# A decoder trunk on one core: first-stage squares and sums moved off GpSimd, attention values as a Strassen product, and several attention steps moved between engines

## The chip, the cores and the metric

The kernel runs on one core of one Trainium2 chip. The metric is the device time of one launch in microseconds (us); the time before is the median of 3 runs. Engines are called PE (TensorE), DVE (VectorE), ACT (ScalarE), POOL (GpSimd) and SP (SyncE, which here only issues DMAs).

## What is computed

The reference is one layer of a decoder trunk on x of 1024 tokens by 1024 channels, float32. Cut to what matters:

```
h = rmsnorm(x, attn_norm_g)
z = h @ w_in            # u, v of a gated MLP; pooling input; q, k, v of attention
gates = sigmoid(h @ w_gate + b_gate)
y_a = gmlp_mixer(u, v)  # gelu, layernorm of v, causal mixing in chunks of 128
y_b = pool_mixer(...)   # running means over 2, 4, 8, 16 tokens
y_c = diff_attn_mixer(q, k, v)   # 4 heads, two softmaxes each, causal
merged = g_a*(y_a@proj_a) + g_b*(y_b@proj_b) + g_c*(y_c@proj_c)
x = x + merged @ w_out
x = x + conv_ffn(rmsnorm(x, ffn_norm_g))
return rmsnorm(x, final_norm_g)
```

## The kernel before

Activations lie with channels on the partitions: `xt[kt]` holds 128 channels by 1024 tokens, and half `j` is 512 tokens. Every float32 operand of a large product is split into a high part (a cast on ACT) and a low part (a subtraction on DVE, `split`, L95), and each product is three matmuls (`mm3`, L187: high by high, high by low, low by high). Large weight products use the Winograd form of Strassen's algorithm, 7 block products for 8 (`strassen_pair`, L251); its operands on the activation side, T1 to T4, are sums of blocks of h, made by `winograd` (L202) from four in-place subtractions and two splits of 128x1024 for each of four pairs of tiles.

The program is written with a tile library: it orders the instructions of each engine by program order, priority and a timeline of its own, and each engine then works through its list in order. Buffers come from pools: `c2` gives 6 buffers of 128x512, `w4` 13 of 128x1024, `a4` 34, and `pb1` and `pm1` give 6 and 2 banks of PSUM.

- **First stage** (L435 to L477). For each half j: the product for u (`pu`, 48 matmuls of 128x512), the product for v (`v_part`, 96 of 128x256, tokens on the partitions), squares of x (`squares`) and from their sums the row factors 1/rms (`factors`, ending in a copy into R8, L344). `bcast_rows` (L146, on PE) spreads R8 along the partitions into RB. `squares` puts even tiles on POOL, odd tiles on ACT (squares) and DVE (sums).
- **Attention values, layer norm, gating** (L581 to L593). `values` multiplies h by the value weights, tokens on the partitions, in 8 pieces of 48 matmuls of 128x256; between the pieces stand `winograd` (three on POOL, one on DVE), `layer_norm` and `gating`.
- **q, k and pooling** (L594 to L618). `strassen_pair` four times; `store_qk` multiplies q and k by RB (`times_r`, on POOL) and splits them. `pooling` is drawn from inside the second pair; `pool_out` (L576, plain float32 matmuls) follows the last of these pairs.
- **Gates** (L686): 12 pairs. **Attention** (L1130 to L1163): 32 tiles of scores, softmax, transposition and product with the values. As filler between tiles, `merge_ab` makes the 32 products with proj_a and proj_b. ACT copies each from PSUM (L1096), POOL multiplies it by its gate (L1097) and adds the pair (L1099). `load_p` splits its weights with the low part on POOL. `attend` takes sums of squares of its result on DVE (L1032). `scores` takes the row minimum of each of up to two chunks on DVE (L675) and joins the two with a reduction (L681).
- Then follow the output product, the feed-forward part and the final norm, which the change leaves as they are.

Of the kernel before, what the change touches and what calls it, by code (L numbers as in the profile page):

```python
# [13 lines left out]
F32R = mybir.dt.float32r  # L14
# [4 lines left out]
P = 128  # L19
# [28 lines left out]
def trunk_kernel(  # L48
# [147 lines left out]
    class Act:  # L196
# [5 lines left out]
        def winograd(self, xt, j, T4=True, eng=None):  # L202
# [3 lines left out]
            e = eng or nc.gpsimd  # L206
# [117 lines left out]
    def squares(kt, j):  # L324

        k = 2 * j + kt % 2
        src = xt[kt][:, half(j)]
        sq = c2("acc" if kt < 2 else "sq")
        if kt % 2 == 0:
            nc.gpsimd.tensor_tensor(out=sq, in0=src, in1=src, op=ALU.mult)  # L330
        else:
            nc.scalar.activation(out=sq, in_=src, func=AF.Square)
        if kt < 2:
            acc[k] = sq
        else:
            (nc.gpsimd, nc.vector)[kt % 2].tensor_tensor(out=acc[k], in0=acc[k], in1=sq, op=ALU.add)

    def factors(j):
        nc.vector.tensor_tensor(out=acc[2 * j], in0=acc[2 * j], in1=acc[2 * j + 1], op=ALU.add)
        ps = pm1()  # L340
        ss_cols(ps, acc[2 * j], 4, 1, 0)
        t = tiny(4, "ssum")
        nc.vector.tensor_scalar(out=t, in0=ps[:, :4], scalar1=1.0 / D, scalar2=1e-6, op0=ALU.mult, op1=ALU.add)
        nc.vector.tensor_copy(R8[:, 4 * j:4 * j + 4], rsqrt(t, 4, j == 0))  # L344
# [62 lines left out]
    def load_V(c):  # L407
        return [list(load_parts(w_tm[1 + c, j].rearrange("p a b -> p (a b)"), 2, True))[0] for j in range(2)]
# [26 lines left out]
    for j in range(2):  # L435
# [28 lines left out]
        else:  # L464
            w_V = [load_V(c) for c in range(2)]
# [4 lines left out]
        bcast_rows(R8[:, 4 * j:4 * j + 4], 4, RB[:, half(j)], pm1)  # L470
# [981 lines left out]
```

## Time and profile before

| | before |
|---|---|
| median of 3 runs | 1421.71 us (1421.44 to 1428.28) |
| the profiled execution | 1421.06 us |
| its span, first to last instruction | 1419.4 us |
| PE / DVE / ACT / POOL busy in the span | 1355.5 / 984.9 / 652.4 / 621.7 us |
| mean granted clock of TensorE | 0.984 |

Busy times are of one profiled execution. Matmuls overlap in the records, so PE's pace is read from the distance of their starts, not from the length of one.

### The profile page before, as it was taken

To read this page: it belongs to the slowest core of one execution; us is meant where nothing else is said; L and a number is where in the kernel's file an instruction comes from. 1 tells how busy PE (TensorE), PEld (TensorE's weight loads), DVE (VectorE), ACT (ScalarE), POOL (GpSimd) and SP (SyncE) were. 2 spreads that over 40 slices of the span, in tenths; PEclk is the share of its full clock that TensorE was granted. 3 is DMA by queue.
4 is the path that set the end of the run, shared out by engine and by line. 5 is a ranking of instruction groups with operands and counts; after the bars stand their busy time and mean duration, and the time that the engine had idled before them with its cause. 6 is when DMAs were issued, how large, how long until landed. Compare 5 with 4: busy or idle time off the path is not lost. (4 is left out here: it accounts for less than half of the span.)

```text
span 1419.4 us, 17845 instructions
## 1 busy us (share of the span) xinstructions
PE 1355.5 (96%) x6502; PEld 1130.4 (80%) x6502; DVE 984.9 (69%) x1502; ACT 652.4 (46%) x1065; POOL 621.7 (44%) x399
## 2 busy tenths in 40 slices
PE   7799999999999889989989999999999999999996
PEld 6699777888888677778868788888888887888786
DVE  8764676454444889976959766677676668985854
ACT  6442244443434666642567433343434335455461
POOL 6523365555544545442132466666666640102014
PEclk9999999999999999999999999999999999999998
DMA  5232044323336986358796122222222247945753
GB/s 188 96 112 90 30 178 151 132 104 119 120 118 173 287 223 185 105 185 191 185 245 159 52 102 77 90 89 74 90 89 74 75 144 273 305 128 151 215 127 119
DMA packets 78256, 200.46 MB, mean 141 GB/s; under 512 B 8206, under 2 KB 17550, under 8 KB 78168
## 3 DMA queue, kind: packets, MB, share of 16 engines
q1 hardware_dynamic: 67800, 180.44, 38.6%
q0 software_dynamic: 10368, 18.88, 7.9%
q8 instruction: 51, 0.84, 0.2%
q14 instruction: 37, 0.30, 0.1%
HBM read 143.70 MB, written 47.46 MB: 135 GB/s over the span
## 5 line engine op out<-in xcount | busy, mean ns | idle before, releaser
L189 PE MATMUL b<-ft,fw 128*128 128x512 f32 (+1 forms) x1308 | 291.7, 383 | 8.3 <-ACT ft L96 3.1
L189 PEld LDWEIGHTS b<-ft,fw 128*128 128x128 f32 x1308 | 238.9, 188 | 58.3 <-ACT ft L96 3.9
L351 POOL TENSOR_TENSOR F<-F,RB 128x1024 f32<-128x1024 f32 x74 | 206.0, 2785 | 145.9 <-DVE F L260 135.4
L189 PE MATMUL b<-hb,Ah 128*128 128x512 f32 x608 | 190.1, 392 | 0.0
L260 DVE TENSOR_TENSOR F<-b,c 128x512 f32<-128x512 f32 x152 | 100.8, 683 | 112.8 <-ACT c L279 68.7
L189 PE MATMUL b<-T,Sh 128*128 128x512 f32 x504 | 155.7, 389 | 1.9 <-ACT c L270 1.9
L232 POOL TENSOR_TENSOR s<-r 128x512 f32<-128x512 f32 x36 | 57.0, 1584 | 200.8 <-DMA r<-in_w_up 96.6
L189 PEld LDWEIGHTS b<-hb,Ah 128*128 128x128 f32 x608 | 114.5, 189 | 24.6 <-issue 1.0
L97 DVE TENSOR_TENSOR Sl<-s,Sh 128x1024 fp32r<-128x1024 f32 x76 | 114.0, 1500 | 26.2 <-PE b L189 22.1
L97 DVE TENSOR_TENSOR Al<-r,Ah 128x1024 fp32r<-128x1024 f32 x38 | 52.6, 1385 | 98.2 <-issue 77.7
L189 PE MATMUL b<-hb,Al 128*128 128x512 f32 x304 | 119.0, 392 | 0.8 <-DVE Al L97 0.8
L96 ACT CAST Sh<-s 128x1024 fp32r<-128x1024 f32 x76 | 80.0, 1052 | 72.8 <-PE b L189 48.6
L189 PEld LDWEIGHTS b<-T,Sh 128*128 128x128 f32 x504 | 94.6, 188 | 21.9 <-ACT c L270 2.4
L189 PE MATMUL b<-hb,Sh 128*128 128x512 f32 x304 | 95.4, 396 | 3.9 <-DVE F L260 3.9
L189 PE MATMUL b<-T,Sl 128*128 128x512 f32 x252 | 98.1, 389 | 0.0
L96 ACT CAST Ah<-r 128x1024 fp32r<-128x1024 f32 x38 | 40.0, 1053 | 110.4 <-PE b L189 106.7
L96 ACT CAST fw<-fr 128x512 fp32r<-128x512 f32 x90 | 54.7, 622 | 64.9 <-DVE fw L97 29.0
L189 PE MATMUL b<-Tl,Sh 128*128 128x512 f32 x204 | 79.4, 389 | 0.0
L189 PE MATMUL b<-Th,Sh 128*128 128x512 f32 x204 | 78.7, 390 | 0.7 <-ACT c L270 0.7
L189 PE MATMUL b<-Th,Sl 128*128 128x512 f32 x204 | 78.6, 389 | 0.0
L104 POOL DMA_DIRECT2D ssb<-sq x24 | 20.7, 876 | 125.8 <-ACT sq L171 37.8
L97 DVE TENSOR_TENSOR A<-r,A 128x512 fp32r<-128x512 f32 x38 | 74.6, 1964 | 0.9 <-ACT A L96 0.9
(260 smaller groups left out, 2982.8 us busy)
## 6 DMA issues: line engine op xcount, KB each, us to landing
fr<-in_w_down SPq DMA_DIRECT2D x47, 512.0 KB, 4.6
r<-in_w_up SPq DMA_DIRECT2D x42, 512.0 KB, 3.5
r<-in_w_gate SPq DMA_DIRECT2D x24, 512.0 KB, 4.1
g_d<-F SPq DMA_DIRECT2D x24, 512.0 KB, 4.8
act_d<-cv SPq DMA_DIRECT2D x22, 512.0 KB, 2.6
act<-act_d SPq DMA_DIRECT2D x22, 512.0 KB, 6.8
fr<-in_w_out SPq DMA_DIRECT2D x18, 512.0 KB, 4.0
ssb<-sq POOLq DMA_DIRECT2D x24, 256.0 KB, 3.9
```

What stands on the lines that cost most here:

```text
L96: nc.scalar.copy(hi, src)
L97: (eng or nc.vector).tensor_tensor(out=lo, in0=src, in1=hi.bitcast(F32), op=ALU.subtract)
L104: nc.gpsimd.dma_start(out=dst, in_=src, accum_op=ALU.add)
L189: nc.tensor.matmul(ps, lhsT=w[a], rhs=x[b], start=first and i == 0, stop=last and i == 2, skip_group_check=more)
L232: eng.tensor_tensor(out=s1[:, :NH], in0=a21, in1=a22, op=ALU.add)
L260: nc.vector.tensor_tensor(out=o, in0=ps, in1=c, op=ALU.add)
L351: (eng or nc.gpsimd).tensor_tensor(out=F, in0=F, in1=RB, op=ALU.mult)
```

## The change

It joins five edits. (1) `squares` puts all squares on ACT and all sums on DVE; `factors` and `bcast_rows` get high priority. (2) All four `winograd` calls are on DVE and stand ahead of the values. (3) `values` becomes one Strassen product of 7 block products of 48 matmuls, with tokens on the partitions; it shares T1 to T4 with the later pairs and needs sums and splits of the value weights, which DVE and ACT make; `layer_norm` and `gating` stand between its steps. (4) `times_r` of the first three q, k pairs is on DVE, and `pool_out` is drawn from inside the first gate pairs. (5) In attention the gate multiplication reads PSUM on DVE, the sum of a pair is an accumulating DMA, the low part of the projection weights is on DVE, the squares are on ACT, and the minimum is carried from one chunk to the next instead of being reduced.

```diff
-        def winograd(self, xt, j, T4=True, eng=None):
+        def winograd(self, xt, j, T4=True):
-            e = eng or nc.gpsimd
+            e = nc.vector
...
-        if kt % 2 == 0:
-            nc.gpsimd.tensor_tensor(out=sq, in0=src, in1=src, op=ALU.mult)
-        else:
-            nc.scalar.activation(out=sq, in_=src, func=AF.Square)
+        nc.scalar.activation(out=sq, in_=src, func=AF.Square)
...
-            (nc.gpsimd, nc.vector)[kt % 2].tensor_tensor(out=acc[k], in0=acc[k], in1=sq, op=ALU.add)
+            nc.vector.tensor_tensor(out=acc[k], in0=acc[k], in1=sq, op=ALU.add)
...
+        with tc.high_priority():
...
...
+        with tc.high_priority():
+            bcast_rows(R8[:, 4 * j:4 * j + 4], 4, RB[:, half(j)], pm1)
...
+    def values():
+        (a11, a12), (a21, a22) = w_V
...
+        def store(o, banks, c, r, i):
+            for b in range(2):
+                TT(out=o[b], in0=banks[b], in1=c[b], op=ALU.add)
...
+        A11, A12 = operand(a11), operand(a12)
+        b1, b2 = ([pb1() for _ in range(2)] for _ in range(2))
+        prod(b1, A11, "B11", True, True)
+        c1 = copies([c2("v") for _ in range(2)], b1)
+        yield
+        s1, s2 = w4(n="s1"), w4(n="s2")
+        TT(out=s1, in0=a21, in1=a22, op=ALU.add)
+        TT(out=s2, in0=s1, in1=a11, op=sub)
+        prod(b2, A12, "B21", True, False)
+        store(c1, b2, c1, 0, 0)
+        S1 = operand(s1)
+        yield
+        b3 = [pb1() for _ in range(2)]
+        prod(b3, S1, "T1", True, True)
+        S2 = operand(s2)
+        TT(out=a21, in0=a11, in1=a21, op=sub)
+        TT(out=a12, in0=a12, in1=s2, op=sub)
+        yield
+        prod(b1, S2, "T2", False, True)
...
+        prod(b1, S3, "T3", False, True)
...
+        prod(b4, A22, "T4", True, False)
...
+        prod(b3, S4, "B22", False, True)
...
-    values(0, (2, 3))
-    h.winograd(xt, 0)
+    for j in range(4):
+        h.winograd(xt, j)
+    vs = values()
+    next(vs)
     layer_norm()
-    values(1, (2, 3))
-    h.winograd(xt, 1, eng=nc.vector)
-    values(0, (0, 1))
-    h.winograd(xt, 2)
+    next(vs)
+    next(vs)
     gating(0)
-    values(1, (0,))
+    next(vs)
     gating(1)
-    h.winograd(xt, 3)
+    next(vs)
+    next(vs)
     wB = prepare(w_qk[0])
-    values(1, (1,))
+    next(vs)
...
-        store_qk(i, strassen_pair(ops, h, pb1, lambda: next(pl, None)))
+        store_qk(i, strassen_pair(ops, h, pb1, lambda: next(pl, None)), nc.vector)
...
-    for f in range(2):
-        pool_out(f, zb[f])
+    po_ = pool_outs()
...
-        Fs = strassen_pair(w_gate[n_], h, pb1)
+        Fs = strassen_pair(w_gate[n_], h, pb1, lambda: next(po_, None))
...
-            nm_ = tiny(1, "nmx")
-            nc.vector.tensor_reduce(out=nm_, in_=mx, axis=AX.X, op=ALU.min)
...
-        nc.vector.tensor_tensor_reduce(out=junk[:, :P], in0=o, in1=o, scale=1.0, scalar=0.0, op0=ALU.mult,
-                                       op1=ALU.add, accum_out=H["ss"][:, i:i + 1])
+        nc.scalar.activation(out=junk[:, :P], in_=po[:, :P], func=AF.Square, accum_out=H["ss"][:, i:i + 1])
...
-    def load_p(m, g, eng=nc.gpsimd):
+    def load_p(m, g, eng=nc.vector):
...
-                    t = c2("pc")
-                    nc.scalar.copy(t, ps)
-                    nc.gpsimd.tensor_tensor(out=g[:, half(j)], in0=t, in1=g[:, half(j)], op=ALU.mult)
+                    nc.vector.tensor_tensor(out=g[:, half(j)], in0=ps, in1=g[:, half(j)], op=ALU.mult)
                     if (g, j) == (gb, 1):
-                        nc.gpsimd.tensor_tensor(out=ga, in0=ga, in1=gb, op=ALU.add)
+                        accumulate(ga, gb)
```

Three places in the engines' lists show how the order moves. The first is DVE before, at the end of the first half's row factors (`hb` are low parts of h, `acc` sums of squares, `rs` the steps of the reciprocal root, `R_93` the table R8):

```order
L317 SCALAR_TENSOR_TENSOR hb_355<-x_92,cs,hb_355 128x512
L336 TENSOR_TENSOR acc_437<-acc_437,sq_490 128x512
L124 RECIPROCAL rs_48_326<-rs_49_327 128x4
L339 TENSOR_TENSOR acc_429<-acc_429,acc_437 128x512
L129 SCALAR_TENSOR_TENSOR rs_49_327<-rs_48_326 128x4
L130 TENSOR_TENSOR rs_49_327<-rs_49_327,ssum_324 128x4
L131 SCALAR_TENSOR_TENSOR rs_48_326<-rs_49_327,rs_48_326 128x4
L344 COPY R_93<-rs_48_326 128x4
```

and the same place now, where the in-place sums for T1 to T4 (`x`) stand between the steps:

```order
L209 TENSOR_TENSOR x_90<-x_90,x_86 128x512
L208 TENSOR_TENSOR x_87<-x_91,x_87 128x512
L212 TENSOR_TENSOR x_89<-x_89 128x512
L130 TENSOR_TENSOR rs_49_327<-rs_49_327,ssum_324 128x4
L212 TENSOR_TENSOR x_90<-x_90 128x512
L208 TENSOR_TENSOR x_88<-x_92,x_88 128x512
L209 TENSOR_TENSOR x_91<-x_91,x_87 128x512
L131 SCALAR_TENSOR_TENSOR rs_48_326<-rs_49_327,rs_48_326 128x4
L209 TENSOR_TENSOR x_92<-x_92,x_88 128x512
L212 TENSOR_TENSOR x_91<-x_91 128x512
L342 COPY R_93<-rs_48_326 128x4
```

Ahead of the copy into R8 DVE's list now holds 15 of these sums and 14 sums of squares, where it held one and 8 (with 16 of `hb`, 8 of the weights' low parts of 128x256 and 2 of 128x1024 both times).

The second place is PE, where `bcast_rows` (`m_407`) waits for that table. Before, it stood inside the second half's product for u:

```order
L189 MATMUL b_421<-hb_343,wh_109 128x512 x2
L189 MATMUL b_421<-hb_343,wl_110 128x512
L189 MATMUL b_422<-hb_343,wh_115 128x512
L146 MATMUL m_407<-ident,R_93 128x128 x4
L189 MATMUL b_422<-hb_343,wh_115 128x512
L189 MATMUL b_422<-hb_343,wl_116 128x512
L189 MATMUL b_421<-hb_346,wh_109 128x512 x2
```

Now it stands behind the whole of it:

```order
L189 MATMUL b_421<-hb_355,wh_109 128x512 x2
L189 MATMUL b_421<-hb_355,wl_110 128x512
L189 MATMUL b_422<-hb_355,wh_115 128x512 x2
L189 MATMUL b_422<-hb_355,wl_116 128x512
L146 MATMUL m_407<-ident,R_93 128x128 x4
L385 MATMUL m_515<-oh_512,rb 4x512
L189 MATMUL b_558<-wh_183,hb_334 128x256
```

What follows it is the product for v of the second half (`b_558`), whose banks come free when ACT has read those of the first half.

The third is DVE now, in the values' stage (`Tl` low parts of T1 to T4, `vg` the v of the gated MLP in its layer norm, `ya` gating, `wl_1055` the low part of the operand of the fifth block product):

```order
L599 TENSOR_TENSOR vg_123<-vg_123,wk_501 128x1024
L599 TENSOR_TENSOR vg_124<-vg_124,wk_501 128x1024
L639 TENSOR_TENSOR ya_977<-m_974,wk_501 64x256 x2
L639 TENSOR_TENSOR ya_984<-m_981,wk_501 64x256 x2
L639 TENSOR_TENSOR ya_991<-m_988,wk_501 64x256 x2
L639 TENSOR_TENSOR ya_998<-m_995,wk_501 64x256 x2
L639 TENSOR_TENSOR ya_1061<-m_1058,wk_501 64x256 x2
L97 TENSOR_TENSOR Tl_736<-x_92,Th_735 128x1024
L639 TENSOR_TENSOR ya_1068<-m_1065,wk_501 64x256 x2
L639 TENSOR_TENSOR ya_1075<-m_1072,wk_501 64x256 x2
L97 TENSOR_TENSOR wl_1055<-wr_495,wh_1054 128x1024
```

The last of the eight splits, `Tl_736`, which the fourth block product needs, stands behind the layer norm and five of eight gating steps; on PE 164 matmuls of the block products stand between the end of the product for v and the first that reads it. Before, no matmul of `values` needed any T.

## Rows read from the trace of the kernel before

**Rows 1.** The page, part 1: busy us, share of the span, instructions of each engine.
```profile
PE 1355.5 (96%) x6502; PEld 1130.4 (80%) x6502; DVE 984.9 (69%) x1502; ACT 652.4 (46%) x1065; POOL 621.7 (44%) x399
```
**Rows 2.** Stretches: length; busy us (instructions) of PE, PEld, DVE, ACT, POOL; clock; DMA.
```profile
0.00:38.80 38.80, 31.09 (x172) 26.33 (x173) 32.17 (x32) 27.39 (x45) 24.96 (x23) 0.91 0.50 172
38.80:76.10 37.30, 30.04 (x172) 24.87 (x171) 27.47 (x51) 13.92 (x25) 14.64 (x14) 0.91 0.32 102
76.10:129.60 53.50, 53.50 (x423) 52.64 (x423) 32.03 (x60) 19.28 (x31) 17.82 (x13) 1.00 0.37 112
...
460.00:640.00 180.00, 159.68 (x925) 135.11 (x924) 151.90 (x486) 112.43 (x272) 83.47 (x54) 0.96 0.68 198
```
**Rows 3.** Waits of PE over the span: us in total, times, longest.
```profile
PE m L146 <- DVE R L344: 7.2, 1, 7.2
PE sc L672 <- DVE mx L675: 5.5, 4, 2.6
...
PE m L576 <- issue: 2.6, 1, 2.6
```
**Rows 4.** Timeline of PE: start us, us, instruction, xcount, [idle before <-releaser].
```profile
18.27 0.79 PE L189 MATMUL b<-hb,wh 128*128 128x512 f32 x1 [4.67 <-DVE hb L317]
...
26.78 0.40 PE L189 MATMUL b<-wh,hb 128*128 128x256 f32 x2
...
27.14 0.40 PE L189 MATMUL b<-wh,hb 128*128 128x256 f32 x2
...
51.19 2.05 PE L146 MATMUL m<-ident,R 128*128 128x128 f32 x8 [7.18 <-DVE R L344]
```
**Rows 5.** DVE instructions by tile, 0 to 60 us: duration ns min/median/max, starts.
```profile
L336 DVE TENSOR_TENSOR acc<-acc,sq x6: 679/1772/1787, 10.7 to 43.7; 128x512 f32<-128x512 f32 x6
...
L317 DVE SCALAR_TENSOR_TENSOR hb<-x,cs,hb x16: 739/1524/1786, 4.9 to 43.0; 128x512 fp32r<-128x512 f32 x16
```
**Rows 6.** Timeline of DVE: the copy into R8, first half and second half.
```profile
49.85 1.19 DVE L344 COPY R<-rs 128x4 f32<-128x4 f32 x1
...
74.71 0.17 DVE L344 COPY R<-rs 128x4 f32<-128x4 f32 x1
```
**Rows 7.** Timeline of ACT at the first gelu.
```profile
57.09 1.28 ACT L427 ACT_TABLE_LOAD   x1
58.39 1.57 ACT L427 ACTIVATE vg<-b,R 128x256 f32<-128x256 f32 x4
```
**Rows 8.** Groups of DVE by form, 60 to 135 us: busy us, mean ns.
```profile
L97 DVE TENSOR_TENSOR Tl<-x,Th 128x1024 fp32r<-128x1024 f32 x8 | 9.9, 1251 | 7.2 <-PE b L189 5.8 <-ACT Th L96 1.0 <-DMA y_d<-uT 0.4
L568 DVE TENSOR_TENSOR ya<-m,wk 64x256 f32<-64x256 f32 x16 | 6.8, 422 | 6.5 <-PE m L561 6.3
L528 DVE TENSOR_TENSOR vg<-vg,wk 128x1024 f32<-128x1024 f32 x4 | 4.6, 1228 | 0.0
...
L523 DVE TENSOR_SCALAR vg<-vg,mv,rs 128x256 f32<-128x256 f32 x8 | 2.7, 413 | 0.0
```
**Rows 9.** Stretches with a lower clock (columns as in rows 2).
```profile
160.00:170.00 10.00, 7.39 (x28) 5.00 (x26) 9.85 (x13) 4.02 (x5) 5.82 (x4) 0.93 0.00 0
170.00:180.00 10.00, 10.00 (x41) 7.95 (x40) 7.06 (x5) 1.64 (x2) 7.44 (x3) 0.90 0.00 0
```
**Rows 10.** Groups of DVE, 460 to 640 us: busy us, mean ns.
```profile
L1002 DVE SCALAR_TENSOR_TENSOR sc<-sc,nr,sc 128x1024 f32<-128x1024 f32 (+3 forms) x16 | 22.1, 1384 | 0.2
L1032 DVE CUSTOM_DVE_ANT_0 sq<-O 128x128 f32<-128x128 f32 x32 | 17.0, 533 | 5.3 <-ACT O L1029 5.3
L1001 DVE SCALAR_TENSOR_TENSOR nr<-nr,s,nlam 128x1 f32<-128x1 f32 x32 | 12.8, 401 | 0.6
L1002 DVE SCALAR_TENSOR_TENSOR sc<-sc,nr 128x256 f32<-128x256 f32 (+3 forms) x16 | 11.3, 713 | 0.4
...
L681 DVE TENSOR_REDUCE nmx<-mx 128x1 f32<-128x2 f32 x32 | 4.7, 148 | 0.1
...
L1122 DVE TENSOR_TENSOR gc<-sc,gc 128x512 f32<-128x512 f32 x3 | 2.1, 689 | 1.0 <-PE sc L189 1.0
```

More of the change, by code (lines that the diff above doesn't have):

```diff
@@ L335, in squares @@
         else:
-            (nc.gpsimd, nc.vector)[kt % 2].tensor_tensor(out=acc[k], in0=acc[k], in1=sq, op=ALU.add)
+            nc.vector.tensor_tensor(out=acc[k], in0=acc[k], in1=sq, op=ALU.add)
     def factors(j):
[L339 to L344, printed above, removed]
+        with tc.high_priority():
+            nc.vector.tensor_tensor(out=acc[2 * j], in0=acc[2 * j], in1=acc[2 * j + 1], op=ALU.add)
+            ps = pm1()
+            ss_cols(ps, acc[2 * j], 4, 1, 0)
+            t = tiny(4, "ssum")
+            nc.vector.tensor_scalar(out=t, in0=ps[:, :4], scalar1=1.0 / D, scalar2=1e-6, op0=ALU.mult, op1=ALU.add)
+            nc.vector.tensor_copy(R8[:, 4 * j:4 * j + 4], rsqrt(t, 4, j == 0))
     def gain(kt):
@@ L405, in load_wide, with load_V @@
         return wk, wsm, pbd
-    def load_V(c):
-        return [list(load_parts(w_tm[1 + c, j].rearrange("p a b -> p (a b)"), 2, True))[0] for j in range(2)]
+    def load_V():
+        r = [[w4(n="wr") for _ in range(2)] for _ in range(2)]
+        for c, k in ((0, 0), (0, 1), (1, 0), (1, 1)):
+            nc.sync.dma_start(out=r[c][k], in_=w_tm[1 + c, k].rearrange("p a b -> p (a b)"))
+        return r
     def evac_fm(dst, ps, j):
@@ L464, in trunk_kernel @@
         else:
-            w_V = [load_V(c) for c in range(2)]
+            w_V = load_V()
             wk, wsm, pbd = load_wide()
@@ L469, in trunk_kernel @@
             pv = [v_part(1, 0)]
-        bcast_rows(R8[:, 4 * j:4 * j + 4], 4, RB[:, half(j)], pm1)
+        with tc.high_priority():
+            bcast_rows(R8[:, 4 * j:4 * j + 4], 4, RB[:, half(j)], pm1)
         u_gelu(j, pu)
@@ L596, in trunk_kernel, with store_qk @@
         times_r(z, nc.vector)
-    def store_qk(i, Fs):
+    def store_qk(i, Fs, eng=None):
         for n_, F in enumerate(Fs):
-            times_r(F)
+            times_r(F, eng)
             hi, lo = a4(dt=F32R, n="qh"), a4(dt=F32R, n="ql")
@@ L613, in trunk_kernel, with pool_outs @@
             pl = pooling(zb)
-        store_qk(i, strassen_pair(ops, h, pb1, lambda: next(pl, None)))
+        store_qk(i, strassen_pair(ops, h, pb1, lambda: next(pl, None)), nc.vector)
     for _ in pl:
         pass
-    for f in range(2):
-        pool_out(f, zb[f])
+    def pool_outs():
+        for f in range(2):
+            for _ in range(2):
+                yield
+            pool_out(f, zb[f])
+    po_ = pool_outs()
     def load_head(hd):
@@ L675, in scores @@
             nc.vector.tensor_tensor_reduce(
-                out=sc_[:, c0:c0 + n], in0=ps[:, :n], in1=H["T"][:, o:o + n], scale=1.0, scalar=3.0e38,
+                out=sc_[:, c0:c0 + n], in0=ps[:, :n], in1=H["T"][:, o:o + n], scale=1.0,
+                scalar=mx[:, 0:1] if n_ else 3.0e38,
                 op0=ALU.add, op1=ALU.min, accum_out=mx[:, n_:n_ + 1])
-        nm_ = mx[:, 0:1]
-        if len(chunks) > 1:
-            nm_ = tiny(1, "nmx")
-            nc.vector.tensor_reduce(out=nm_, in_=mx, axis=AX.X, op=ALU.min)
+        nm_ = mx[:, n_:n_ + 1]
         sum_ = H["s0"][:, i:i + 1] if c == 0 else tiny(1, "s1")
```

62 lines of the change are left out of this document (47 added, 15 removed).

## Prediction, written before the changed kernel ran

> **What bounds the kernel now.** I read the page's busy shares first. PE works 96% of the span [rows 1], so time comes only from matmuls left out, from places where PE idles, and from stretches with a low clock. A table of stretches [rows 2] says where these are: from the start to the end of the product for v (76.1 us) PE is busy 61.1 of 76.1 us at a clock of 0.91; the values' stage to 129.6 us is solid, PE busy all 53.5 us at full clock; the attention stretch (460 to 640 us) leaves 20.3 of its 180 us idle, with DVE busy 151.9. The list of PE's waits [rows 3] names the places that the change touches: 7.2 us for the table R8, 2.6 us ahead of `pool_out`, 5.5 us in four waits for row minima. PE's timeline [rows 4] dates two: 4.67 us until 18.27 for a low part of h, and 7.18 us until 51.19, where `bcast_rows` wants R8. From it comes PE's pace as well: three matmuls of 128x256 start in 0.36 us (26.78 to 27.14), 0.12 each; one of 128x512 I count as two.
>
> Why DVE is late there shows in its own rows [rows 5]: adding squares to a sum takes 0.68 us at best and 1.77 us in the median, the low part of h 0.74 to 1.79. Even the tiny copy into R8 takes 1.19 us in the first half and 0.17 in the second [rows 6]. POOL is busy 25 of the first 38.8 us, 14.6 of the next 37.3 [rows 2]; I read the long ones as DVE waiting on POOL's accesses to SBUF.
>
> **Part 1, start to the end of v.** DVE's list ahead of R8 now has 16 low parts of h at 0.74 (11.8), 8 low parts of weights of 128x256 at about 0.41 (3.3; L523 has that size [rows 8]), 2 of 128x1024 at 1.25 (2.5), 14 sums of squares at 0.68 (9.5), 15 sums for T1 to T4 at 0.68 (10.2) and some 5 tiny steps at 0.17 (0.9): 38.2 us, at the prices that DVE has without POOL, whose squares, sums and T1 to T4 all leave this stage. It starts at 4.9 [rows 5]; with 3 us of waiting for x and ACT (8 more squares there, some 5 us beside 41 busy of 76 [rows 2]) R8 is ready near 46. PE starts its first half's product 3 us sooner (the low parts come at 0.74 instead of 1.5), ends it near 23, then makes v of one half (96 x 0.12 = 11.5) and u of the other (48 x 0.24 = 11.5), and wants R8 near 46. The wait of 7.2 goes; 4.67 becomes about 1.5. What is late next: v of the second half needs banks that ACT frees with its gelu, behind R8: spreading and copy 1.3, table load 1.28 and two pairs of gelu 0.8 [rows 7], 3.4 us together, which did not show before because u's last matmuls stood behind `bcast_rows`. Then 96 matmuls with the small ones of the factors, 14.5. End of v: 46 + 3.4 + 14.5 = 64 instead of 76.1: **-12**. Ends: 0 if R8 comes 12 us late, -16 if nothing of the 3.4 shows.
>
> **Part 2, the values.** 7 x 48 matmuls for 8 x 48: 48 x 0.12 = 5.8 us saved if nothing else stopped PE. But before, no matmul here needed T1 to T4; now the fourth block product needs the last low part, which stands behind in DVE's list: from the end of v, the second half's factors (4.2, tiny steps and what stands between), statistics of v (2.3), u times RB (1.3), two additions for a stored block (1.4), eight splits (9.9), layer norm (2.7 + 4.6), five pairs of gating (10 x 0.42 = 4.2), all by [rows 8] where they have a row there, and some 2 of tiny steps: about 32 us. PE has 164 matmuls before it (19.7), the spreading (0.6) and seven gating products (4.7): 25 us. So PE waits about 7 us in pieces, and with pieces of idleness comes a lower clock; from 160 to 180 us, behind a hole of 2.6, the granted clock was 0.93 and 0.90 [rows 9], a mean between the two levels of 1.2 and 2.4 GHz, which cost 0.7 + 1.0 = 1.7 us. I put 1 on it. -5.8 + 7 + 1 is **+2**. Ends: -5.8, nothing waited for; and +11, if every split also waits for its cast on ACT (8 x 1.05 for them beside the 32).
>
> **Part 3, q, k and pooling.** `times_r` of six tensors of 128x1024 goes to DVE at 1.23 (a multiplication of that size [rows 8]), 7.4 us in a stage where DVE is far from full; POOL loses as many. `pool_out` between block products no longer stands in a row that nothing prepared: its wait of 2.6 [rows 3] and the low clock behind it, 1.7, go: **-4**. Ends: 0 and -4.3. The sums of value weights that DVE and ACT make lie beside PE's 25 us.
>
> **Part 4, attention.** DVE loses 32 squares (17.0) with their reads (some 2.6), 32 joins of minima (4.7) [rows 10]; it gains 32 gate multiplications of 128x512 from PSUM at 0.69 (L1122 is one such [rows 10]), 22 us, and 8 low parts at 0.69, 5.5. Its balance by count is +3. POOL, however, loses nearly all its 83.5 us of this stretch [rows 2], and what DVE pays for POOL can be read: L1001 on one column takes 401 ns where tiny steps take 170 [rows 6], 32 x 0.23 = 7.4; L1002 takes 22.1 + 11.3 = 33.4 us for 16 + 16 instructions whose eight lengths of 128 to 1024 columns add up to 18,432 columns, that is 36 times 512; at 0.69 each [rows 10] 25, so 8 less at least, 16 if the smaller tensors were inflated most. DVE would be busy 151.9 + 3 - 20 = 135 of 180 us. ACT sheds 32 copies and gains 32 squares, about nothing. PE idles here because DVE delivers late: I take 9 of the 20.3 us back, near half, since the waits for minima (5.5) and some others end at DVE but a chain of small steps stays: **-9**. Ends: 0 and -20.
>
> Here the Trainium skill speaks against the change: its page Perfetto Trace Analysis, section Optimizing Scalar/DVE Operations, says that moving work between GPSIMD and DVE might not help, as they share a port to SBUF, and that DVE's access costs some 125 ns on PSUM against 60 ns on SBUF. By that the 32 multiplications from PSUM would cost 2 us more, an estimate from that page. The trace shows 689 ns for L1122 from PSUM and 679 for a sum from SBUF, which leaves no such difference. That the port is held by one engine at a time (page SBUF - State Buffer, section SBUF: two separate sides) agrees with 679 against 1772.
>
> **Sum.** -12 + 2 - 4 - 9 = -23. The profiled execution took 1421.06 us around a span of 1419.4, 0.65 below the median of the runs, 1421.71. So about **1398 us**. The order after attention is the same, and I count nothing there.
>
> **Rivals.** (a) The values run free: the splits come in time, because DVE falls idle before the end of v and pulls them forward. Then part 2 is -5.8 and the time 1390. For it: DVE does 9.9 us of splits in 53 now and waits 7.2 for PE there [rows 8]. Against: layer norm stands ahead in the list. 0.15. (b) Attention gains nothing, as DVE's 32 added multiplications take what POOL gives back: 1398 + 9 = 1407. For it: the balance by count is +3, and the relief is inferred. This is also what the skill's rule on offloading would give. 0.20. (c) R8 is as late as before, since 29 sums stand ahead of it: a wait of 7.2 remains, 1405. For it: ACT must scale all of x before those sums can be made. 0.10. (d) Slower: DVE becomes the bound in attention. Each of the 32 products with proj_a and proj_b then holds its bank until DVE comes to it, and PE stands for it as it stands now for a row minimum, 5.5 / 4 = 1.4 us a time [rows 3]: 32 x 1.4 = 44 us over (b), 1451. It decides once DVE has over about 165 us of work in 180; it has 151.9 now, 155 by count if POOL's absence gives nothing. 0.06. (e) Gains and waits cancel, 1415 to 1422: 0.04.
>
> **How the numbers follow.** My forecast has 0.45. The range that should hold 8 in 10 runs from 1384 (case (a) with the better ends of parts 1 and 4) to 1414 (case (b) with half of part 1 lost); it leaves out (d), (e) and the far ends. About 0.5%, 7 us here, is what a measurement of this kernel can tell from no change. Faster by more than that (below 1414.6) are the forecast, (a), (b) and (c) except for their bad ends: 0.86; within it, (e) and some of (b): 0.07; slower, (d) and some sum of bad ends: 0.07.
>
> **What would show it.** Right: the wait for R8 gone and the product for v ended near 64; sums on DVE at 0.68 throughout the first 45 us; 528 matmuls of 128x256 in v and values instead of 576; new waits of PE in 64 to 100 for `Tl`, `vg` and `ya` of some 7 us; DVE near 135 us busy in the attention stretch, its L1001 near 0.2, and PE's idle time there near 11. Wrong: a wait at `bcast_rows` of several us (part 1), waits of PE for the merge's multiplications (part 4), a clock below 0.95 over the values' stage (part 2), or time moved in the stages behind attention, which I left at nothing.

## The result and the profile after

The median is 1402.22 us in 4 runs (1400.68 to 1405.20) for 1421.58 of the kernel before. The medians lie 19.4 us apart; the ratio over all the runs of both is 0.9855 (95% interval 0.9822 to 0.9889). The forecast was 1398. The profiled execution took 1400.68 us, its span 1399.0. Its busy time by engine, for [rows 1]:

```profile
PE 1347.8 (96%) x6454; PEld 1120.9 (80%) x6454; DVE 962.8 (69%) x1481; ACT 654.0 (47%) x1110; POOL 502.3 (36%) x327
```

POOL lost 119 us, PE 8. Where the 20.4 us of the span went is read from the time at which PE reaches the same instruction in both kernels. PE's instructions by tile give it (the two numbers ahead of the semicolon are the first and the last start), here of the kernel after:

```profile
L516 PE MATMUL b<-wh,hb x4: 283/283/363, 62.7 to 72.2; 128*128 128x256 f32 x4
...
L189 PE MATMUL b<-hb,Ah x608: 389/389/478, 119.3 to 1150.2; 128*128 128x512 f32 x152
...
L189 PE MATMUL b<-Th,Sl x204: 388/389/389, 123.9 to 450.9; 128*128 128x512 f32 x102
...
L189 PE MATMUL b<-ft,fw x1308: 277/389/502, 656.7 to 1385.5; 128*128 128x512 f32 x174, 128*128 128x256 f32 x13
```

and of the kernel before:

```profile
L189 PE MATMUL b<-hb,Ah x608: 387/389/1415, 129.5 to 1166.1; 128*128 128x512 f32 x152
...
L189 PE MATMUL b<-Th,Sl x204: 388/389/397, 132.7 to 461.9; 128*128 128x512 f32 x102
...
L189 PE MATMUL b<-ft,fw x1308: 278/389/502, 670.1 to 1405.4; 128*128 128x512 f32 x174, 128*128 128x256 f32 x13
```

The first `b<-hb,Ah` opens the first q, k pair, the last `b<-Th,Sl` is the end of the q, k and gate pairs, the first `b<-ft,fw` opens the output product. The differences (the first two stages part at 76.1 before, at 62.7 after):

| stage | before | after | difference | forecast |
|---|---|---|---|---|
| start to the end of v | 76.1 | 62.7 | -13.4 | -12 |
| values | 53.4 | 56.6 | +3.2 | +2 |
| q, k, pooling, gates | 332.4 | 331.6 | -0.8 | -4 |
| attention and merge | 208.2 | 205.8 | -2.4 | -9 |
| output product to the end | 749.3 | 742.3 | -7.0 | 0 |

So the total came close, but its terms failed in opposite directions: 10 us that were forecast for pooling and attention did not come, and 7 came where none were counted.

The stretches, for [rows 2] (length; busy us and instructions of PE, PEld, DVE, ACT, POOL; clock; DMA):

```profile
0.00:62.70 62.70, 56.68 (x338) 48.57 (x339) 45.65 (x91) 42.06 (x69) 2.90 (x10) 1.00 0.45 157
62.70:119.30 56.60, 51.65 (x378) 48.33 (x377) 41.85 (x76) 25.22 (x40) 11.57 (x12) 0.97 0.31 103
...
451.00:528.00 77.00, 61.56 (x335) 49.22 (x333) 57.98 (x157) 40.79 (x106) 7.09 (x4) 0.91 0.88 245
528.00:612.00 84.00, 82.14 (x515) 70.83 (x514) 75.94 (x254) 58.85 (x181) 4.30 (x5) 1.00 0.75 194
```

The first stage runs at full clock with POOL out of it. The values' stage, solid before, has 5 us of PE idle and a clock of 0.97. Attention falls in two: an opening of 77 us with 15.4 us of PE idle and a clock of 0.91 (1.2 GHz for a part of it), and the rest, nearly solid. PE's longest waits, for [rows 3]:

```profile
PE b L189 <- DVE F L260: 8.0, 2, 6.6
PE m L647 <- DVE F L622: 3.6, 1, 3.6
PE mm L189 <- ACT ph L96: 3.2, 1, 3.2
PE m L632 <- DVE vg L599: 2.9, 1, 2.9
```

The wait for R8 is gone, and so are the row minima from the head of the list. In their place stand 6.6 us at a bank that DVE's sum `F` frees, 3.6 us in `pool_out`, 2.9 us for `vg`, which are taken apart below, and 3.2 us for `ph` in the merge. PE's timeline at each:

```profile
44.68 1.05 PE L146 MATMUL m<-ident,R 128*128 128x128 f32 x8
...
48.56 0.39 PE L189 MATMUL b<-wh,hb 128*128 128x256 f32 x1 [1.88 <-ACT vg L428]
...
87.87 5.38 PE L632 MATMUL m<-wpp,vg 128*128 128x256 f32 x16 [2.94 <-DVE vg L599]
93.43 1.99 PE L632 MATMUL m<-wpp,vg 128*128 128x256 f32 x8 [0.18 <-DVE ya L639]
95.57 1.10 PE L632 MATMUL m<-wpp,vg 128*128 128x256 f32 x4 [0.15 <-DVE ya L639]
97.37 0.39 PE L189 MATMUL b<-wh,Tl 128*128 128x256 f32 x1 [0.69 <-DVE Tl L97]
...
158.49 3.78 PE L647 MATMUL m<-F,wpp 128*128 128x512 f32 x4 [3.61 <-DVE F L622]
...
457.95 1.22 PE L189 MATMUL b<-hb,Sh 128*128 128x512 f32 x2 [6.64 <-DVE F L260]
...
509.00 2.07 PE L189 MATMUL mm<-yv,ph 128*128 128x512 f32 x4 [3.18 <-ACT ph L96]
```

### The profile page after: what moved, and what is told of

It is laid out like the page before. It is cut to its first block, busy times and chain, and to the rows that moved or that the text cites. A ratio compares the mean times of both kernels' runs of the same rounds, so it can differ in the third digit from the quotient of the medians.

```text
span 1399.0 us, 17655 instructions
## 1 busy us (share of the span) xinstructions
PE 1347.8 (96%) x6454; PEld 1120.9 (80%) x6454; DVE 962.8 (69%) x1481; ACT 654.0 (47%) x1110; POOL 502.3 (36%) x327
## 4 chain that ended last, share of the span: by engine, by line
PE 38%; DVE 6%; DMA 3%; issue 2%; ACT 1%; POOL 0%; DVEq 0%; SPq 0%; ACTq 0%; POOLq 0%
PE b L189 38%; DMA fr<-in_w_down 1%; DMA x<-in_xT 1%; DVE fw L97 1%; DMA act<-act_d 1%; DVE Sl L97 0%; DMA x_d<-x 0%; DVE T L97 0%; DVE ft L97 0%; DVE x L908 0%; DVE hb L999 0%; DVE x L1326 0%; ACT fw L96 0%; DVE Al L97 0%; DVE fr L879 0%
## 5 line engine op out<-in xcount | busy, mean ns | idle before, releaser
L349 POOL TENSOR_TENSOR F<-F,RB 128x1024 f32<-128x1024 f32 x68 | 192.3, 2830 | 125.6 <-DVE F L260 124.0
L97 DVE TENSOR_TENSOR Al<-r,Ah 128x1024 fp32r<-128x1024 f32 x38 | 50.0, 1315 | 151.5 <-issue 75.7
L189 PEld LDWEIGHTS b<-hb,Ah 128*128 128x128 f32 x608 | 114.0, 188 | 23.6
L97 DVE TENSOR_TENSOR Sl<-s,Sh 128x1024 fp32r<-128x1024 f32 x76 | 96.5, 1270 | 6.8 <-ACT Sh L96 6.7
L97 DVE TENSOR_TENSOR A<-r,A 128x512 fp32r<-128x512 f32 x38 | 79.6, 2094 | 0.0
L189 PEld LDWEIGHTS b<-hb,Sh 128*128 128x128 f32 x304 | 58.5, 193 | 22.4 <-DVE F L260 8.8
```

What stands on the lines that cost most here:

```text
L97: (eng or nc.vector).tensor_tensor(out=lo, in0=src, in1=hi.bitcast(F32), op=ALU.subtract)
L189: nc.tensor.matmul(ps, lhsT=w[a], rhs=x[b], start=first and i == 0, stop=last and i == 2, skip_group_check=more)
L349: (eng or nc.gpsimd).tensor_tensor(out=F, in0=F, in1=RB, op=ALU.mult)
```

## The experiments

### The first stage alone, and POOL's part in it

The first kernel is that of before with edit 1 of the change and, of edit 2, `winograd` on DVE (its calls stay between the pieces of the values), and nothing else.

```diff
-            e = eng or nc.gpsimd
+            e = nc.vector
...
-        if kt % 2 == 0:
-            nc.gpsimd.tensor_tensor(out=sq, in0=src, in1=src, op=ALU.mult)
-        else:
-            nc.scalar.activation(out=sq, in_=src, func=AF.Square)
+        nc.scalar.activation(out=sq, in_=src, func=AF.Square)
...
-            (nc.gpsimd, nc.vector)[kt % 2].tensor_tensor(out=acc[k], in0=acc[k], in1=sq, op=ALU.add)
+            nc.vector.tensor_tensor(out=acc[k], in0=acc[k], in1=sq, op=ALU.add)
...
+        with tc.high_priority():
...
```

> The kernel before, with the first stage alone changed: all squares on ACT, all sums of squares and all of T1 to T4 on DVE, priority for the factors and the spreading; values, pooling and attention as before. Theory: POOL's accesses made DVE's work two to three times longer there, and taking them away ends the product for v 13.4 us sooner; nothing later gives it back, so 1421.5 - 13.4 = 1408 us (1406 to 1411). Rival: most of the gain is in what the rest of the change does with T1 to T4, and the values' stage, which now has DVE busy with the sums, gives 5 us or more back: 1413 to 1418.

Measured: 1409.05 us, 0.9917 of before (0.9892 to 0.9942). It opens its first q, k pair at 117.9 us, 11.6 sooner than before, and the stages behind it keep their lengths within a few us. The gain of part 1 of the prediction stays; none of it needs the rest of the change. The three things that this kernel joins (squares and sums off POOL, `winograd` off POOL, priority for the factors) were not run apart.

Is it POOL's accesses that made DVE slow, or that the two shared tiles? The next two kernels are the changed one with work on POOL that touches nothing else, and DVE, ACT and PE lists that are the same to the row.

```diff
+    junk_ = a4(n="jk")
+    nc.gpsimd.memset(junk_, 1.0)
+    for _ in range(24):
+        nc.gpsimd.tensor_tensor(out=junk_[:, :NH], in0=junk_[:, NH:], in1=junk_[:, NH:], op=ALU.mult)
```

> The changed kernel with 24 products of 128x512 added on POOL at the start, each reading and writing a buffer that nothing else uses; the lists of DVE, ACT and PE are the same to the row. Theory: POOL's accesses to SBUF alone make DVE's instructions with two inputs from SBUF two to three times longer: over the first 35 us the sums of squares and the low parts of h take 1.5 to 1.8 us instead of 0.7, R8 comes 8 us or more later, and the kernel takes 1410 us (1406 to 1415). Rival: before, DVE was slow because it shared tiles with POOL (squares to add, sums to wait for), which this kernel does not do: 1400 to 1404, sums at 0.7.

```diff
+    for _ in range(48):
+        nc.gpsimd.memset(junk_[:, :NH], 2.0)
```

> The changed kernel with 48 fills of 128x512 (memset) added on POOL at the start, which write a buffer that nothing else uses and read none; lists of DVE, ACT and PE the same to the row. Theory: what slowed DVE in the run with 24 products on POOL (first stage 14 us longer) was POOL reading SBUF through a port that it shares with DVE; fills only write, and DVE's sums stay at 0.68 to 0.8 us: 1400 to 1405. Rival: any work of POOL on SBUF holds the port, and the sums take 1 us or more while it lasts: 1407 to 1420, according to how long the fills last.

Measured: 1415.68 us with the products (0.9965 of before, 0.9947 to 0.9983), just above the theory's range, and 1402.76 with the fills (0.9887, 0.9848 to 0.9925), the changed kernel's own time. DVE's sums of squares and POOL's added work by tile (duration in ns min/median/max, first and last start), with the products:

```profile
L333 DVE TENSOR_TENSOR acc<-acc,sq x12: 682/1103/1525, 13.7 to 48.0; 128x512 f32<-128x512 f32 x12
...
L375 POOL TENSOR_TENSOR jk<-jk x24: 1040/1366/1371, 2.3 to 32.5; 128x512 f32<-128x512 f32 x24
```

with the fills:

```profile
L333 DVE TENSOR_TENSOR acc<-acc,sq x12: 672/682/778, 10.5 to 34.1; 128x512 f32<-128x512 f32 x12
...
L375 POOL MEMSET jk<- x48: 524/526/534, 2.3 to 29.7; 128x512 f32 x48
```

and in the changed kernel:

```profile
L333 DVE TENSOR_TENSOR acc<-acc,sq x12: 678/682/779, 10.9 to 34.2; 128x512 f32<-128x512 f32 x12
```

Products on POOL, on data that nobody else uses, take back all of part 1: the first q, k pair opens at 133.0 us, later than before the change (129.5). PE loses the time at the low parts of h, which DVE makes (median 1056 ns for 742 in the changed kernel), and at `bcast_rows` it does not wait:

```profile
PE b L189 <- DVE hb L317: 11.5, 3, 8.8
```

Fills (48 x 526 ns, 25 us in all, for 33 us of products) do nothing at all. What the second theory named holds: a reading POOL instruction holds DVE up, a writing one does not. The Trainium skill says so (SBUF - State Buffer, section SBUF: two separate sides): an instruction of DVE with two inputs from SBUF and a GpSimd instruction that reads SBUF exclude each other for their whole length. These two runs agree with it.

### The opening of attention

Why does PE wait 6.6 us at 457.95? ACT's timeline of the changed kernel:

```profile
448.19 0.30 ACT L773 ACTIVATE lam<-lam,zero 128x2 f32<-128x2 f32 x1
455.00 1.04 ACT L96 CAST yv<-yr 128x1024 fp32r<-128x1024 f32 x1 [6.51 <-DMA yr<-y_d]
455.95 0.58 ACT L279 COPY c<-b 128x512 f32<-128x512 f32 x1
```

and DVE's:

```profile
456.07 1.23 DVE L97 TENSOR_TENSOR yv<-yr,yv 128x1024 fp32r<-128x1024 f32 x1 [7.21 <-ACT yv L96]
457.22 0.68 DVE L260 TENSOR_TENSOR F<-b,c 128x512 f32<-128x512 f32 x1
```

A cast for the merge (`yv`, the split of y_a) stands in ACT's list ahead of the copy `c` of the last q, k pair. Its data come by a DMA at 455.0, so ACT stands 6.5 us, the copy with it, behind it DVE's sum `F`, and PE at the bank that `F` frees. The next kernel holds the cast back:

```diff
-        nc.scalar.copy(c_3, b1)
+        MK["c3"] = nc.scalar.copy(c_3, b1)
...
-            yab = [load_yab(i) for i in range(4)]
+            with tc.issue_after(MK["c3"].ins):
+                yab = [load_yab(i) for i in range(4)]
```

> The changed kernel, with one thing held back: the splits of y_a and y_b for the merge (yv) stand on ACT and DVE behind the last copy of c_3 in the last q, k pair, instead of ahead of it. Theory: at the opening of attention ACT stands 6.5 us at a cast of yv whose data are not there, the copy of c_3 queues behind it, DVE's sum F behind that, and PE waits 6.6 us for the bank, with a low clock behind the hole (0.91 over 451 to 528 us). Then this kernel has no such wait and takes about 1402 - 6.6 - 2 = 1393 us (1390 to 1397). Rival: the opening is short of work anyway, and the later casts only move the hole to the merge's first products: 1400 to 1404.

Measured: 1389.35 us, 0.9783 of before (0.9764 to 0.9803; the interval of the changed kernel ends above it, at 0.9822), 12.9 under the median of the changed kernel. The copy now stands first (lines are 2 higher in this kernel):

```profile
452.03 0.59 ACT L281 COPY c<-b 128x512 f32<-128x512 f32 x1 [2.87 <-PE b L191]
452.51 1.05 ACT L98 CAST yv<-yr 128x1024 fp32r<-128x1024 f32 x1
```

and attention takes 193.3 us for 205.8. That is 4 us more than the wait and the clock that were expected to go: the two stretches of attention, to be held against those of the changed kernel above,

```profile
452.00:530.00 78.00, 72.25 (x414) 61.45 (x415) 69.18 (x198) 51.43 (x137) 10.28 (x6) 0.93 0.95 268
530.00:612.00 82.00, 80.27 (x490) 68.30 (x488) 67.91 (x222) 53.96 (x166) 4.63 (x6) 1.00 0.77 211
```

show PE with 10.7 us more of work done in the opening (72.25 in 78 us for 61.56 in 77), at a clock of 0.93. Beside the wait for `F`, which fell to 1.40 us, the 3.18 for `ph` at 509.00 is gone too; it stood in the same opening and was not counted.

### Part 5 with the opening mended

Against this kernel the worth of part 5 of the change (part 4 of the prediction) can be measured. The first kernel takes all of it back, the second the merge alone (its gate multiplications, pair sums and the low part of its weights).

Both:

```diff
-    def load_p(m, g, eng=nc.vector):
+    def load_p(m, g, eng=nc.gpsimd):
...
-                    nc.vector.tensor_tensor(out=g[:, half(j)], in0=ps, in1=g[:, half(j)], op=ALU.mult)
+                    t = c2("pc")
+                    nc.scalar.copy(t, ps)
+                    nc.gpsimd.tensor_tensor(out=g[:, half(j)], in0=t, in1=g[:, half(j)], op=ALU.mult)
...
-                        accumulate(ga, gb)
+                        nc.gpsimd.tensor_tensor(out=ga, in0=ga, in1=gb, op=ALU.add)
```

The first alone:

```diff
-                scalar=mx[:, 0:1] if n_ else 3.0e38,
+                scalar=3.0e38,
...
+            nc.vector.tensor_reduce(out=nm_, in_=mx, axis=AX.X, op=ALU.min)
...
-        nc.scalar.activation(out=junk[:, :P], in_=po[:, :P], func=AF.Square, accum_out=H["ss"][:, i:i + 1])
+        nc.vector.tensor_tensor_reduce(out=junk[:, :P], in0=o, in1=o, scale=1.0, scalar=0.0, op0=ALU.mult,
+                                       op1=ALU.add, accum_out=H["ss"][:, i:i + 1])
```

> The changed kernel with y_a's and y_b's splits held back, and with the attention of before: copy by ACT, gate multiplication, sum of a pair and low part of the projection weights on POOL, squares on DVE, minimum joined by a reduction. Theory: with the opening mended, part 5 of the change is worth the difference between the attention stretches of the two kernels, 208.2 - 193.3 = 15 us: 1389.4 + 14 = 1403 us (1399 to 1407), DVE's steps of one column back from about 0.2 to 0.4 us. Rival: the mended opening makes up most of it, and part 5 alone is worth under 5 us: 1390 to 1394.

> The changed kernel with y_a's and y_b's splits held back, and only the merge as before (copy by ACT, multiplication, sum and low part of the projection weights on POOL); squares stay on ACT, the minimum stays carried. Theory: what helps is POOL's absence from SBUF, not the instructions that DVE is spared: DVE loses 32 multiplications here and still gets slower per instruction, 1389.4 + 10 = 1399 us (1396 to 1404). Rival: it is the chain, which the squares and the joins of the minimum made longer, and this kernel keeps it short: 1389 to 1392.

Measured: 1412.91 us with all of part 5 taken back (0.9942 of before, 0.9924 to 0.9961) and 1416.69 with the merge alone (0.9966, 0.9950 to 0.9983). So against the old attention part 5 is worth 23.6 us, more than either theory gave, and all of it is the merge: with that on POOL, squares on ACT and the carried minimum gain nothing (1416.69 with them, 1412.91 without). A part of the 23.6 is not the price of part 5 as such: the old attention takes 215.7 us here for 208.2 in the kernel before, with 13.9 us of waits for row minima for 5.5; why, no run shows. DVE's groups over attention, with the merge on DVE (the kernel with the mended opening; busy us, mean ns),

```profile
L1080 DVE SCALAR_TENSOR_TENSOR sc<-sc,nr,sc 128x1024 f32<-128x1024 f32 (+3 forms) x16 | 17.3, 1082 | 0.2
...
L1171 DVE TENSOR_TENSOR gb<-mm,gb 128x512 f32<-128x512 f32 x16 | 11.0, 687 | 0.7 <-PE mm L191 0.4
...
L1079 DVE SCALAR_TENSOR_TENSOR nr<-nr,s,nlam 128x1 f32<-128x1 f32 x32 | 6.9, 216 | 0.5
```

and with the merge on POOL:

```profile
L1080 DVE SCALAR_TENSOR_TENSOR sc<-sc,nr,sc 128x1024 f32<-128x1024 f32 (+3 forms) x16 | 23.0, 1436 | 0.4
L1079 DVE SCALAR_TENSOR_TENSOR nr<-nr,s,nlam 128x1 f32<-128x1 f32 x32 | 21.3, 665 | 0.8
```

The step on one column takes 665 ns for 216 in the mean. By tile (duration in ns min/median/max) and in time, with the merge on POOL:

```profile
L1078 DVE RECIPROCAL nr<-s x32: 147/159/165, 462.3 to 611.5; 128x1 f32<-128x1 f32 x32
L1079 DVE SCALAR_TENSOR_TENSOR nr<-nr,s,nlam x32: 206/220/2154, 463.4 to 611.6; 128x1 f32<-128x1 f32 x32
...
503.74 3.36 POOL L1175 TENSOR_TENSOR ga<-ga,gb 128x1024 f32<-128x1024 f32 x1
...
504.77 0.15 DVE L1078 RECIPROCAL nr<-s 128x1 f32<-128x1 f32 x1
504.96 2.15 DVE L1079 SCALAR_TENSOR_TENSOR nr<-nr,s,nlam 128x1 f32<-128x1 f32 x1
```

The median is 220 ns, as with the merge on DVE; 14 of the 32 take 333 to 2154 ns. Each of these 14 began while a product or a pair sum ran on POOL and ended 14 to 19 ns after that one's end. The reciprocal just ahead, with one input, never takes over 165 ns, though POOL works beside 15 of the 32. So DVE's step with two inputs from SBUF waits for the end of the POOL instruction that runs. In the kernel before all its 8 long steps (425 to 1315 ns) end 16 to 21 ns after the end of a POOL product as well.

These steps stand in the chain from the scores to the transposition that PE waits for, and their 14 us are the largest growth of any group of DVE. Attention is 21.0 us longer with the merge on POOL (214.3 for 193.3), and 13.8 of them are idle time of PE (21.4 us for 7.6). That DVE's steps make the greater part of it is argued: PE's waits there end at several instructions of DVE and ACT, and ACT too has more to do, 32 copies (127.8 us busy for 113.2), which no run separates from POOL's part. The 32 multiplications that DVE makes in return (687 ns each, 22 us) are not in that chain.

### The values and their buffer

Why do the layer norm and the gating stand ahead of `Tl_736` in DVE's list? T1 to T4, the blocks of h, x, `uT`, `vg` and two tables share one pool of 34 buffers; counted, the last low part is the 35th. It has a place only when the gating of the first half is stored. The next kernel gives the pool one more, paid for by the small buffers.

```diff
-    cp = ctx.enter_context(tc.tile_pool(name="cp", bufs=6))
+    cp = ctx.enter_context(tc.tile_pool(name="cp", bufs=4))
...
-    ap_ = ctx.enter_context(tc.tile_pool(name="ap", bufs=34))
+    ap_ = ctx.enter_context(tc.tile_pool(name="ap", bufs=35))
```

> The changed kernel with one more buffer of 128x1024 in the pool that holds T1 to T4 (35 for 34, paid for by 4 instead of 6 small buffers of 128x512). Theory: the last low part stands behind layer norm and five gating steps on DVE because it has no buffer before the gating of the first half has been stored; with a buffer, DVE's list has all eight low parts ahead of the layer norm, PE's seven gating products no longer stand in front of the fourth block product, and the values' stage (56.6 us, 5 of them waits and 5 more in gating products that wait for banks) takes about 52: 1402 - 4.6 = 1397.6 us (1395 to 1400). Rival: DVE's sum of work is the limit whatever its order, and the waits come back at the sums of the value weights: 56 us and 1401 to 1404.

Measured: 1392.90 us, 0.9808 of before (0.9787 to 0.9828). The list has the eight low parts ahead of the layer norm, and the first q, k pair opens at 104.1 us for 119.3: 15 us, not 5. From the opening of the output product to that of the feed-forward part it takes 114.1 us for 103.9, however, so I gave the buffer a pool of its own that ends with the last q, k pair, once alone and once with the opening of attention mended:

```diff
+    cpool.append(st1.enter_context(tc.tile_pool(name="cp1", bufs=4, reuse_waits="tile")))
+    tx = st1.enter_context(tc.tile_pool(name="tx", bufs=1, reuse_waits="tile"))
...
-                t4, t2 = op2(u, a4, "T")
+                t4, t2 = op2(u, a4, "T", tlow if j == 3 else None)
...
     st1.close()
+    cpool.append(ctx.enter_context(tc.tile_pool(name="cp", bufs=6, reuse_waits="tile")))
```

> The changed kernel with the one buffer more for T1 to T4, in a pool that lives to the end of the last q, k pair, and nothing held back at the opening of attention. Theory: the buffer alone takes some 15 us out of the values' stage, and 5 of them come back later (2 to 3 between the first pair and attention, 3 behind it), as between the two mended kernels, 1389.4 and 1380.6: 1402.2 - 9 = 1393 us (1390 to 1396), with the wait of PE at the opening of attention still there if the order there is the same. Rival: the 4 small buffers of the run with 35 buffers were what changed attention (199.8 for 205.8 us), so this one gains more, 1386 to 1389, or without them the order gives all back, 1399 to 1402.

> The changed kernel with both mends: the splits of y_a and y_b held behind the last copy of c_3, and one more buffer for T1 to T4, this time in a pool of its own that lives only to the end of the last q, k pair (with 4 small buffers till there and 6 behind). Theory: the two gains are in different stages and add: 1389.4 for the first, less the 15 us by which the run with 35 buffers reached its first q, k pair sooner (104.1 for 119.3), and 1 or 2 given back by the scarcer small buffers: 1375 us (1372 to 1379). Rival: the loss of that run after attention (114.1 for 103.9 us to the first product of the feed-forward part) is not from its 4 small buffers but follows from reaching that place sooner, at loads that are no sooner there: 1383 or more.

Measured: 1385.17 us for the buffer alone (0.9751, 0.9715 to 0.9787), 17 under the changed kernel and less than the theory's 1390, and 1380.61 for both (0.9708, 0.9682 to 0.9734), the lowest median of all, though the two intervals overlap. The values' stage of the latter (61.6 us is the start of its first block product, 104.8 that of the first q, k pair):

```profile
61.60:104.80 43.20, 42.91 (x330) 41.65 (x329) 38.06 (x68) 21.76 (x31) 12.23 (x11) 1.00 0.29 93
```

PE is solid at full clock. But the 15 us are not all gained: the first pair opens before the values are done. The last of their seven block products stands behind that opening:

```profile
104.80 0.63 PE L191 MATMUL b<-hb,Ah 128*128 128x512 f32 x2
...
108.00 0.28 PE L191 MATMUL b<-wh,hb 128*128 128x256 f32 x1
```

In the changed kernel all seven end ahead of it. With these 48 matmuls (5.8 us at 0.12) the values take 49.0 us, for 56.6 in the changed kernel and 53.4 before.

The two mends do not add: with the buffer alone the order at the opening of attention came out right by itself, the copy `c` ahead of the cast, and PE's wait there is 1.46 us for 6.64:

```profile
439.29 0.72 PE L189 MATMUL b<-hb,Sh 128*128 128x512 f32 x2 [1.46 <-DVE F L260]
```

So the bad place of that cast is an accident of the list, not a property of the change. What the forecast for both (1375) lacked went behind attention. By the end of the gates 13.4 us are gained on the kernel with the opening mended (438.2 for 451.6): the pairs and gates take 333.4 us for 330.8, with the 5.8 us of the moved product in them. From the output product on it is 749.2 us for 742.7, of which the output product takes 109.7 for 106.5.

Does the Strassen product pay at all, as the change has it? The last kernel of this group has the opening mended and the values of before:

```diff
-    vs = values()
-    next(vs)
+    values(0, (2, 3))
+    h.winograd(xt, 0)
     layer_norm()
-    next(vs)
-    next(vs)
+    values(1, (2, 3))
+    h.winograd(xt, 1)
...
```

> The changed kernel with y_a's and y_b's splits held back, and with the values of before (8 pieces of 48 matmuls that need no T1 to T4; the sums for T1 to T4 stay on DVE, between the pieces as before). Theory: as the change was built, the Strassen product saves 5.8 us of matmuls and gives more than that back in waits for T1 to T4 and the gating; with the old values the first q, k pair begins near 117.9 us, as in the run with only the first stage changed, for 120.8 with the product: 1389.4 - 2 = 1387 us (1384 to 1391). Rival: the sums for T1 to T4 between the pieces cost DVE and PE what the product saves, so the old values are slower: 1393 to 1397.

Measured: 1400.54 us, 0.9870 of before (0.9830 to 0.9910). In the stage itself the theory holds: the first q, k pair opens at 115.8 us, 5 sooner than with the product (120.8). Over the whole it fails: attention then took 199.8 us for 193.3, and the stages from the output product on 751.5 for 742.7. The loss lies in stages that the values do not touch, so this run does not price the product. With one buffer more it pays: there the first pair opens at 104.8, 110.6 with the moved block product counted, for 115.8 here. The order in attention is another, and a wait of 4.2 us for a row minimum is in it; what the values have to do with the last stages is taken up below.

### The product of the pooling

`pool_out` was drawn from inside the gate pairs, but in PE's list its first products stood inside the second q, k pair, as soon as the list's maker held them ready. The next kernel moves them behind it.

```diff
+        MK[i] = MK["mm"]
...
-            pool_out(f, zb[f])
+            with tc.issue_after(MK[f].ins):
+                pool_out(f, zb[f])
```

> The changed kernel with the plain float32 products of the pooling held on PE behind the whole of the first and the second q, k pair; they stand 12 matmuls later in PE's list. Theory: the wait of 2.6 us and the low clock of before were not removed but moved; PE waits 3.6 us at the first of them for the pooled tile and runs at 0.84 and 0.81 for 20 us. Without the wait the time is 1402 - 3.6 - 3 = 1395.5 us (1394 to 1399). Rival: the low clock is not from the hole but from the plain float32 products themselves: then only the wait goes, 1398.5, and the clock stays near 0.8 in those 20 us.

Measured: 1401.26 us, 0.9860 of before (0.9838 to 0.9882): neither. The wait for the pooled tile went, and PE stands in its place at a bank, for DVE's sum `F` (all of PE's waits from 120 to 180 us):

```profile
PE b L191 <- DVE F L262: 4.2, 1, 4.2
```

DVE is full there. In the changed kernel the stretches around it read:

```profile
150.00:160.00 10.00, 6.39 (x24) 4.55 (x23) 9.83 (x13) 5.16 (x7) 5.46 (x3) 0.84 0.00 0
160.00:170.00 10.00, 10.00 (x35) 7.15 (x34) 7.24 (x9) 0.59 (x1) 0.00 (x0) 0.81 0.00 0
```

DVE is busy 9.83 of 10 us in the first, mostly with the pooling's sums, and in both orders PE waits for one of its results; the granted clock falls to a mean between its two levels in both stretches, as after the hole of before [rows 9]. In the kernel with both mends the same wait is 2.0 us, and the clock stays at 1.00 from 140 to 170 us.

## Why the prediction came out as it did

**Part 1 (-12, measured -13.4): right, with its mechanism.** Sums of squares at 0.68 us throughout, R8 ready at 42.7 (46 forecast), no wait at `bcast_rows`. The 3.4 us behind R8 that were forecast as newly visible are 3.9, from the start of the spreading at 44.68 to the product for v at 48.56; 1.88 of them PE waits, the spreading itself and two small products for the bias of attention (`oh`, `rb`) fill the rest. The added products on POOL show the cause: they alone take the stage back.

**Part 2 (+2, measured +3.2): the size nearly right, the mechanism half.** The forecast had PE wait about 7 us for DVE's sum of work, 32 us against 25. The waits are there: 2.94 for `vg`, 8.8 us for seven gating products that were put at 4.7, and 0.69 for `Tl`, 7.7 us together. But DVE's sum was not the limit. The step "the last low part, which stands behind in DVE's list" took the list as given; it stood there for want of one buffer, and with it PE is solid beside nearly the same work of DVE (38.1 us busy in 43.2, for 41.9 in 56.6). Then the values take 4.4 us less than before, for the 5.8 that the left-out product is worth. Rival (a), given 0.15, names that outcome; it was one buffer away, though not by the means that I named.

**Part 3 (-4, measured -0.8): wrong.** "No longer stands in a row that nothing prepared" was concluded from where the code draws `pool_out`, not from PE's list, where it stands inside the second q, k pair. The wait became 3.6 us for 2.6, and the clock behind it fell lower, 0.84 and 0.81 for 0.93 and 0.90. The run with it moved shows the deeper error: the term was booked as PE's, but DVE is full there, and to move the product only moved the wait.

**Part 4 (-9, measured -2.4): wrong in the sum, too small in the mechanism.** Alone it is worth -14.9 (attention 208.2 to 193.3 us with the opening mended), and 23.6 us on the whole kernel against the old attention in its place. Two errors partly cancelled. Only half of PE's idle time was taken back because "a chain of small steps stays": but POOL's instructions hold up that chain, and its 32 steps on one column went from 401 to 216 ns in the mean (the sum had taken 170 for their own price). And the opening, where a cast slipped ahead of a copy, is not in the sum at all; it cost 12.9 us. Rival (b), attention gains nothing, fits the number of this stage and not the cause. The rule of the Trainium skill that I weighed there (Perfetto Trace Analysis, section Optimizing Scalar/DVE Operations: moving work between GPSIMD and DVE might not help, as they share a port) says only that it might not help. In the direction of this change it did, by 27 us for the merge alone, and the 14 steps that end with POOL's instructions show what DVE was freed from. Rival (d), DVE as the bound, did not come: it was busy 143 of 179 us, for 135 of 180 forecast.

**The rest (0, measured -7.0): wrong, and mostly open.** PE's list behind the merge is the same in both kernels, row for row. The gain is in waits of 1 to 2.5 us, those above 0.4 us sum to 15.5 before and 10.2 after, and in the clock that they cost. The largest piece that can be placed is 2.8 us at the turn to the last product: PE's wait for `F` there is 2.50 us before and 1.33 after, and the granted clock over these ten and seven us 0.83 and 1.00.

```profile
1179.70:1189.80 10.10, 7.61 (x27) 5.75 (x27) 8.83 (x11) 4.33 (x7) 0.00 (x0) 0.83 0.56 177
...
1163.80:1171.10 7.30, 5.97 (x27) 4.61 (x25) 6.78 (x9) 3.71 (x6) 0.00 (x0) 1.00 0.59 176
```

This piece goes with the values: it takes 10.0, 9.8 and 9.2 us in the three kernels with the old ones (before, first stage alone, mended opening with old values) and 7.0 to 7.3 in the ten with the Strassen product, with the old attention or the new. The stretch behind it does not: 229.3, 229.4 and 232.7 us for 226.7 to 231.6. That the assignment of buffers, which the values shift, decides which load waits for which release is a guess; no run tested it.

The total was near for a poor reason: -10 us of forecasts that failed (parts 3 and 4) against -7 that nobody forecast.

## What to carry to other kernels

To take reading work off POOL is worth more than POOL's share of the time says: DVE's instructions with two inputs from SBUF, and the tiny ones in a latency chain most of all, get back the time that they stood behind POOL. After a joint change, read the list of each engine at the seams between stages, not only where code was edited: one instruction that waits for a load, ahead of one that frees a bank, cost here 12.9 us, as much as part 1 gained. And where a list puts late work ahead of urgent work, count the buffers before blaming the engine: one more was worth 7.6 us in the values (49.0 for 56.6) and 17 on the kernel.

## What the runs showed of the hardware

A step on 128 x 1 elements with two inputs from SBUF took 216 ns in the mean with the merge off POOL and 665 ns beside a POOL that multiplies and adds. The mean hides two cases: 18 of 32 kept their 206 to 223 ns, and 14 waited out the POOL instruction that was running, up to 2154 ns. A reciprocal of the same size, with one input, kept its 147 to 165 ns throughout. 48 fills on POOL, 25 us of them beside DVE's first 30 us, cost DVE nothing. An addition of 128x512 took 682 ns from SBUF, a multiplication with one input from PSUM 687 ns, no difference that matters.
